# A two-block transformer kernel: the state space mixer's second half is prepared behind the first half's inputs, its pace is halved, and conditioning tiles are spread into GLU and w_out

## The chip, the cores and the metric

The kernel runs on one core of one Trainium2 chip, in one launch. The metric is the device time of that core in microseconds, taken as the median of several executions. The engines are named as the profile names them: PE is TensorE (matmuls and transposes; PEld its weight loads), DVE is VectorE, ACT is ScalarE, POOL is GpSimd, SP is SyncE, which issues the DMAs of the weights. Each works through its own list of instructions in order. A matmul of f32 operands shows in the trace as two passes.

## What is computed

Two transformer blocks follow each other on 256 tokens of width 2048, in f32. The change lies in the first block. Cut to it, the reference is:

```python
mod = silu(c) @ w_ada + b_ada                      # conditioning: 2048 x 12288
shift1, scale1, gate1, shift2, scale2, gate2 = split(mod, 6)
h = rms(x, norm1_w) * (1 + scale1) + shift1
u, q, k, v = split(h @ w_in, 4)                    # in-projection, 1024 columns each
# state space mixer: 64 groups of 16 channels, 64 complex states each
abar = exp((a_re + i a_im) * dt); bbar = (abar - 1) / a * b
h_t = abar * h_(t-1) + bbar u_t                    # over the 256 tokens
y = gelu(Re(c h_t) + d * u)
y_ssm = y * sigmoid(y @ w_glu)                     # GLU, 1024 x 1024
y_att = dilated_attention(rms(q), rms(k), v)       # 8 heads of 128
x = x + gate1 * (concat(y_ssm, y_att) @ w_out)
h2 = rms(x, norm2_w) * (1 + scale2) + shift2
x = x + gate2 * ((silu(h2 @ w_gate) * (h2 @ w_up)) @ w_down)
# the second block (attention mixer, then Fourier mixer) follows
```

## The kernel before

**What it does in which order.** The program is a straight line of instructions that Python writes out. Up to the FFN of the first block it has these stages: load x, norm and first modulation; the in-projection (`turns(ada_group(g), in_tiles(..))`), which reads w_in tile by tile; the evacuation of u (L977); attention, in which `rest(n)` finishes q, k and v, `normed` scales and transposes q and k (L997 to L1006), and `scores` and `values` run eight heads; the attention half of w_out (`gemm_full`, L1072); GLU (`gemm` on `ssm_w_glu`, L1078 to L1089); the SSM half of w_out with the residual (L1101 to L1105); the norm (L1108 to L1116), the second modulation's transposes (`modulated2`, L457) and the FFN.

**Lanes.** Side work is written as Python generators, called lanes. `tick(f)` (L195) adds `f * rate` to each lane's account, and the lane emits pieces until the costs that it yields have used that up. `until(mark)` emits a lane up to a named mark, and `finish()` emits all that is left. So a rate decides how much side work the main line gets between two of its own tiles; each engine then runs its share in the order written. From the evacuation of u to GLU the main line makes 48 ticks: six `rest` calls, eight heads of two half ticks, and 16 tiles of w_out.

**The lane "ada"** brings the conditioning matrix for the later modulations in tiles of 0.5 MB. A first kind (`ada_gen`, loads at L306) is added up on DVE with the token's coefficient (`ada_add`, L278). A second kind (`ada_quad`, loads at L353) goes through PE as four matmuls of 32 rows against `cz` (L133), and is turned by transposes (`ada_turn`, L317). Gate 1 must be there before w_out's residual (`until("g1")`), shift 2 and scale 2 before the FFN (`until("m2")`). Its rate is `T["ada"]` per tick up to GLU and `T["ada2"]` after.

**The lane "ssm"** is the mixer. `products(half)` (L609 to L624) forms powers of abar times bbar on DVE and spreads them by ACT; `expand_b(half)` (L636, L638) transposes them into the input matrices; `outward()` (L647 to L654) prepares c by transposes; `kernel_of(half)` (L664 to L677) multiplies both on PE in 64 passes of 32 columns, then ACT copies the result (L672) and DVE adds d to it (L675, L677). All this needs only parameters, and stands ahead of the mark "prep", at which the lane waits till the in-projection's last group. After u is there, `chunked` (L687) lays it out, `inputs(half)` (L697) makes the input terms with 64 passes of 64 columns, `scan` (L713, L715) runs 63 steps on DVE, `chunk_kernel` (L706) and `outward_powers` (L729 to L737) go along with it, and `outputs` (L753) writes y. Its rate there is `T["ssm"]`.

**Weights.** w_in, w_glu and the SSM half of w_out mostly come through `wtile` (L214): ACT casts the tile to its upper part (L177), DVE subtracts for the lower (L178), and PE makes three products of each. `full_tile` (L207) loads weights that are used as plain f32. Tiles of the lane "ada" and of `wtile` share one set of five buffers, `raw`, and SP's queue.

In the changed kernel lines from 765 on stand one or more lines further down (L1002 there is L1001 here).

Of the kernel before, what the change touches and what calls it, by code (L numbers as in the profile page):

```python
# [20 lines left out]
A_SCALE = 192.0 ** -0.5  # L21
B_SCALE = 128.0 ** -0.5
TWO_PI = 6.283185307179586
T = dict(groups=((0, 2), (2, 6), (6, 10), (10, 14), (14, 16)), db=(0, 6), us=(3,4),qs=(), hf=0.5, raw=5, sl=14, side=[[0, 1, 2, 3], [0, 1, 2, 3], [0, 1, 2], [0, 1, 2], []], ada0=0.0, ada=1.8, ssm0=0.6, ssm=5, md=(2, 2), ld=(3, 3), stg=(7, 7), r1=(0, 0), ada2=0.2, prep=1.6, hb=0.75, ha=1.5, cx=0.6)


class Act:
# [54 lines left out]
def kernel(ctx: ExitStack, tc: tile.TileContext, A, out):  # L82
# [20 lines left out]
    def slab(shape, dt=F32):  # L103
        return sl.tile(shape, dt, name=uname("sl"), tag="sl", bufs=NSLAB)
# [398 lines left out]
    def ssm():  # L503
# [94 lines left out]
        exs, kst, bls, us = {}, {}, {}, {}  # L598

        def products(half):  # L600


            pr = slab([128, 4, 256])
            ex = exs[half] = [w8([128, 16, 4, 2, 16]) for _ in range(2)]
            f = lambda a: a.rearrange("p (g c) -> p g c", c=16)

            def cmul(dr, di, ar, ai, br, bi):
                t1 = temp()
                V.tensor_tensor(out=f(dr), in0=f(br), in1=by_pair(ar, half), op=ALU.mult)  # L609
                V.tensor_tensor(out=f(t1), in0=f(bi), in1=by_pair(ai, half), op=ALU.mult)  # L610
                V.tensor_tensor(out=dr, in0=dr, in1=t1, op=ALU.subtract)
                V.tensor_tensor(out=f(di), in0=f(bi), in1=by_pair(ar, half), op=ALU.mult)
                V.tensor_tensor(out=f(t1), in0=f(br), in1=by_pair(ai, half), op=ALU.mult)
                V.tensor_tensor(out=di, in0=di, in1=t1, op=ALU.add)
            for j in range(4):
                d = [pr[:, 2 * (j % 2) + comp] for comp in range(2)]
                if j == 0:
                    cmul(*d, sm[:, 2], sm[:, 3], bb[:, half, 0], bb[:, half, 1])
                else:
                    cmul(*d, sm[:, 0], sm[:, 1], *last)  # L620
                last = d
                for comp in range(2):
                    for g in range(2):
                        S.activation(out=ex[comp][:, :, 3 - j, g], in_=f(d[comp]), func=AF.Copy,  # L624
                                     scale=maskb[:, g:g + 1])
                yield 2.0

        def expand_b(half):

            bls[half] = []  # L630
            for comp in range(2):
                bt = w8([128, 16, 128])
                for q in range(4):
                    b = ps_tp()
                    for i in range(4):
                        PE.transpose(b[:, i * 128:(i + 1) * 128],  # L636
                                     exs[half][comp][:, 4 * q + i].rearrange("p j g c -> p (j g c)"), ident)
                    S.copy(bt[:, 4 * q:4 * q + 4].rearrange("p g n -> p (g n)"), b)  # L638
                bls[half].append(bt)
                yield 0.5  # L640

        def outward():

            for comp in range(2):
                for half in range(2):
                    cx = w2([128, 4, 2, 64], "wb")
                    S.activation(out=cx, in_=cn[:, comp, 4 * half:4 * half + 4].unsqueeze(2).to_broadcast([128, 4, 2, 64]),  # L647
                                 func=AF.Copy, scale=(1.0, -1.0)[comp])
                    b = ps_tp()
                    for kk in range(4):  # L650
                        PE.transpose(b[:, kk * 128:(kk + 1) * 128], cx[:, kk].rearrange("p g n -> p (g n)"), ident)
                    for g in range(2):
                        r_ = slice(64 * g, 64 * g + 64)
                        S.copy(gc[r_, comp, 16 * half:16 * half + 16],  # L654
                               b[r_].rearrange("p (k g c) -> p k g c", g=2, c=16)[:, :, g])
                    yield 0.5

        def kernel_of(half):

            ct = []  # L660
            for comp in range(2):
                ct.append(w2([128, 16, 2, 16], "wb"))
                for g in range(2):
                    S.activation(out=ct[comp][:, :, g], in_=gc[:, comp, 16 * half:16 * half + 16], func=AF.Copy,  # L664
                                 scale=maskb[:, g:g + 1])
            b = ps_at()
            for q in range(16):
                for comp in range(2):
                    mm(b[:, 32 * q:32 * q + 32], exs[half][comp][:, q].rearrange("p j g c -> p (j g c)"),
                       ct[comp][:, q].rearrange("p g c -> p (g c)"), comp == 0, comp == 1)  # L670
            k = kst[half] = sp.tile([128, 16, 32], F32, name=uname("ssm_k"), tag="ssm_k", bufs=2)
            S.copy(k.rearrange("p q n -> p (q n)"), b)  # L672
            l0 = slice(96, 128)
            dd = w2([128, 16, 32], "wb")
            V.tensor_tensor(out=dd[l0], in0=ident[l0, 96:128].unsqueeze(1).to_broadcast([32, 16, 32]),  # L675
                            in1=dcol[l0, 16 * half:16 * half + 16].unsqueeze(2).to_broadcast([32, 16, 32]), op=ALU.mult)
            V.tensor_tensor(out=k[l0], in0=k[l0], in1=dd[l0], op=ALU.add)  # L677
            yield 2.0

        def chunked(half):  # L680

            us[half] = slab([128, 16, 64])
            for i in range(4):
                for q in range(4):
                    d = us[half][32 * i:32 * i + 32].rearrange("p (k q) n -> p q k n", q=4)[:, q]
                    copy = (S.copy, V.tensor_copy)[q % 2]
                    copy(d, uT[half][32 * q:32 * q + 32, :, i:256:4])  # L687

        def inputs(half):

            for comp in range(2):
                for h8 in range(2):
                    b = ps_at()
                    for q in range(8):
                        mm(b[:, q * 64:(q + 1) * 64], bls[half][comp][:, 8 * h8 + q], us[half][:, 8 * h8 + q], True, True)
                    g0 = 16 * half + 8 * h8
                    S.copy(st[:, :, comp, g0:g0 + 8].rearrange("p n g -> p g n"), b.rearrange("p (g n) -> p g n", g=8))  # L697
# [22 lines left out]
        def outward_powers():  # L720

            for half in range(2):
                gx[half] = [w8([128, 16, 4, 2, 16]) for _ in range(2)]
                gr, gi = (gc[:, comp, 16 * half:16 * half + 16] for comp in range(2))
                ar, ai = by_pair(sm[:, 0], half), by_pair(sm[:, 1], half)
                f = lambda a: a.rearrange("p (g c) -> p g c", c=16)
                for j in range(4):
                    t1, t2 = temp(), temp()
                    V.tensor_tensor(out=f(t1), in0=gi, in1=ai, op=ALU.mult)  # L729
                    V.tensor_tensor(out=f(t2), in0=gr, in1=ai, op=ALU.mult)  # L730
                    V.tensor_tensor(out=gr, in0=gr, in1=ar, op=ALU.mult)
                    V.tensor_tensor(out=gi, in0=gi, in1=ar, op=ALU.mult)
                    V.tensor_tensor(out=gr, in0=gr, in1=f(t1), op=ALU.add)
                    V.tensor_tensor(out=gi, in0=gi, in1=f(t2), op=ALU.subtract)
                    for comp, g_ in enumerate((gr, gi)):
                        for g in range(2):
                            S.activation(out=gx[half][comp][:, :, j, g], in_=g_, func=AF.Copy, scale=maskb[:, g:g + 1])  # L737
                    yield
# [19 lines left out]
        dcol = tmp[:, 0]  # L758
        for q in range(4):
            V.tensor_copy(dcol[96:128].rearrange("p (k q) -> p q k", q=4)[:, q], colv[32 * q:32 * q + 32, C_D:C_D + 8])  # L760
        gc = slab([128, 2, 32, 16])
        yield from outward()
        for half in range(2):
            yield from products(half)
            yield from kernel_of(half)
            if half == 0:
                yield from expand_b(0)
        yield "prep"

        st = sp.tile([128, 64, 2, 32], F32, name=uname("ssm_h"), tag="ssm_h", bufs=2)  # L770
# [1 line left out]
        for i in range(1, 4):  # L772
            G.memset(tk[32 * i:32 * i + 32, :, :, 0:i].rearrange("p h q j c -> p (h q) (j c)"), 0.0)
        chunked(0)
        inputs(0)
        yield 1.0
        chunked(1)
        yield from expand_b(1)
        inputs(1)
        powers = outward_powers()  # L780
        yield 1.0
        for c, cost in enumerate(scan()):
# [1016 lines left out]
```

## Time and profile before

| | us |
|---|---|
| median of three runs | 2521.72 |
| lowest and highest of them | 2508.95, 2525.09 |
| the profiled execution | 2516.57 |
| its span | 2514.6 |
| its mean granted clock of PE | 0.975 |

The rows are read from the profiled execution. Times within it count from the start of its span. A row of windows gives, for a stretch, the busy time of each engine with its number of instructions, PE's granted clock as a share of full speed (2.4 GHz; 0.50 is the lower level), and the load of DMA. The chain of waits follows the work that ended last back through what released it.

### The profile page before, as it was taken

How to read it: one execution, taken by the hardware profiler on the slowest of the kernel's cores; microseconds unless marked ns; L12 is line 12 of the kernel's file. 1: busy time of each engine (PE TensorE's matmuls, PEld its weight loads, DVE VectorE, ACT ScalarE, POOL GpSimd, SP SyncE). 2: the span in 40 equal slices, each digit the busy share in tenths (PEclk: the TensorE clock that was granted, in tenths of full speed). 3: DMA queues.
4: the chain of work that ended last, by engine and by line, in shares of the span. 5: the costliest groups of instructions: out<-in, count | busy, mean ns of one | idle time of the engine just before them, and what ended most of it. 6: DMA issues, size and time to landing. Idle time of an engine off the chain costs nothing.

```text
span 2514.6 us, 30153 instructions
## 1 busy us (share of the span) xinstructions
PE 2379.3 (95%) x10791; PEld 1826.3 (73%) x10791; DVE 1768.4 (70%) x2809; ACT 1127.4 (45%) x1770; POOL 5.6 (0%) x7
## 2 busy tenths in 40 slices
PE   5899999989999999999999999999997999999997
PEld 3456645567888778778777878777776778888886
DVE  5876795477668899886777789645678655555557
ACT  3334835355444333434345464555444445444442
POOL 0000000000000000000000000000000000000000
PEclk9888999999999999999999999999998999999999
DMA  9867587877888888888777998634473765665664
GB/s 291 307 241 268 192 300 244 287 253 258 282 272 289 279 290 287 272 257 276 260 250 229 294 302 282 216 102 149 126 261 108 229 212 173 190 198 156 176 209 139
DMA packets 291535, 591.32 MB, mean 235 GB/s; under 512 B 33733, under 2 KB 56617, under 8 KB 291385
## 3 DMA queue, kind: packets, MB, share of 16 engines
q1 hardware_dynamic: 291384, 589.40, 72.1%
q8 instruction: 84, 1.38, 0.2%
q14 instruction: 67, 0.54, 0.1%
HBM read 587.19 MB, written 2.13 MB: 234 GB/s over the span
## 4 chain that ended last, share of the span: by engine, by line
PE 52%; DVE 20%; DMA 18%; issue 5%; ACT 4%; SPq 0%; DVEq 0%; ACTq 0%
PE mm L133 41%; DMA raw<-in_ada_w_dram 14%; PE at L133 7%; DVE wl L178 6%; DVE acc L278 6%; PE tp L133 2%; ACT wh L177 1%; DMA raw<-in_w_ada_dram 1%; DMA raw<-in_w_ffn_down_dram 1%; DMA raw<-in_w_in_attn_dram 1%; PE tp L189 1%; DVE ssm_h L715 1%; DVE wa L278 0%; DVE sl L1570 0%; DVE sl L1573 0%
## 5 line engine op out<-in xcount | busy, mean ns | idle before, releaser
L133 PE MATMUL mm<-wh,s 128*128 128x512 f32 (+3 forms) x4768 | 1464.8, 386 | 2.5 <-ACT wh L177 2.2
L177 ACT CAST wh<-raw 128x1024 fp32r<-128x1024 f32 (+3 forms) x642 | 655.8, 1023 | 900.3 <-PE mm L133 653.4
L133 PEld LDWEIGHTS mm<-wh,s 128*128 128x128 f32 x4768 | 891.4, 189 | 181.8 <-issue 8.6
L178 DVE TENSOR_TENSOR wl<-raw,wh 128x1024 fp32r<-128x1024 f32 (+3 forms) x642 | 756.3, 1186 | 321.0 <-ACT wh L177 319.3
L133 PE MATMUL mm<-wl,s 128*128 128x512 f32 (+3 forms) x2384 | 923.3, 387 | 23.2 <-DVE wl L178 21.4
L278 DVE SCALAR_TENSOR_TENSOR acc<-raw,condT,acc 128x1024 f32<-128x1024 f32 (+2 forms) x413 | 477.7, 1165 | 235.9 <-DMA raw<-in_ada_w_dram 146.4
L133 PEld LDWEIGHTS mm<-wl,s 128*128 128x128 f32 x2384 | 451.3, 189 | 124.6 <-DVE wl L178 38.9
L133 PE MATMUL mm<-wh,sl 128*128 128x512 f32 x536 | 196.2, 459 | 4.5 <-ACT sl L817 2.8
L133 PE MATMUL mm<-wl,sl 128*128 128x512 f32 x440 | 194.9, 521 | 4.3 <-DVE wl L178 2.3
L133 PEld LDWEIGHTS mm<-wh,sl 128*128 128x128 f32 x536 | 100.5, 191 | 56.5 <-issue 32.4
L133 PEld LDWEIGHTS mm<-wl,sl 128*128 128x128 f32 x440 | 82.2, 193 | 68.5 <-issue 51.3
L133 PE MATMUL tp<-wc,sl 128*128 128x128 f32 (+1 forms) x352 | 49.3, 293 | 20.0 <-ACT wc L901 15.3
L133 PEld LDWEIGHTS tp<-wc,sl 128*128 128x128 f32 x352 | 44.9, 199 | 29.8 <-ACT wc L901 15.6
L278 DVE SCALAR_TENSOR_TENSOR wa<-raw,condT,wa 128x512 f32<-128x512 f32 (+1 forms) x75 | 48.2, 642 | 10.1 <-DMA raw<-in_w_ada_dram 9.3
L133 PE MATMUL at<-wl,sl 128*128 128x512 f32 x112 | 52.4, 617 | 0.5 <-DVE sl L864 0.5
L133 PE MATMUL at<-s,s 128*128 128x512 f32 (+1 forms) x96 | 44.8, 647 | 3.9 <-ACT wd L1381 3.3
L133 PEld LDWEIGHTS at<-wl,sl 128*128 128x128 f32 x112 | 21.3, 198 | 26.6 <-issue 21.5
L133 PE MATMUL at<-wh,sl 128*128 128x512 f32 x80 | 36.0, 597 | 0.0
L457 PE MATMUL tp<-ident,sl 128*128 128x128 f32 x64 | 12.0, 337 | 22.7 <-ACT sl L1594 10.5
L189 PEld LDWEIGHTS tp<-ident,wa 128*128 128x128 f32 x208 | 24.5, 141 | 10.4 <-issue 3.3
L189 PE MATMUL tp<-ident,wa 128*128 128x128 f32 x208 | 30.5, 276 | 0.0
L715 DVE TENSOR_TENSOR ssm_h<-ssm_h,ssm_tq 128x64 f32<-128x64 f32 x126 | 27.6, 219 | 1.4
(345 smaller groups left out, 1725.2 us busy)
## 6 DMA issues: line engine op xcount, KB each, us to landing
raw<-in_w_ada_dram SPq DMA_DIRECT2D x192, 512.0 KB, 5.3
raw<-in_ada_w_dram SPq DMA_DIRECT2D x192, 512.0 KB, 4.6
raw<-in_w_in_fourier_dram SPq DMA_DIRECT2D x128, 512.0 KB, 4.1
raw<-in_w_ffn_gate_dram SPq DMA_DIRECT2D x88, 512.0 KB, 4.9
raw<-in_w_ffn_up_dram SPq DMA_DIRECT2D x88, 512.0 KB, 4.7
raw<-in_w_ffn_down_dram SPq DMA_DIRECT2D x88, 512.0 KB, 5.6
raw<-in_w_in_attn_dram SPq DMA_DIRECT2D x72, 512.0 KB, 5.1
raw<-in_w_out_fourier_dram SPq DMA_DIRECT2D x64, 512.0 KB, 4.0
```

The costliest lines, as they stand in the source:

```text
L133: PE.matmul(o, l, r, start=start, stop=stop)
L177: S.copy(hi, src)
L178: V.tensor_sub(lo, src, hi.bitcast(F32))
L189: PE.transpose(b[:, o:o + 128], src(c0 + c, t), ident)
L278: V.scalar_tensor_tensor(out=acc, in0=raw, scalar=c, in1=acc, op0=ALU.mult, op1=ALU.add)
L457: PE.transpose(b[:, c * 128:(c + 1) * 128], xn(4 * g + c, t), ident)
L715: V.tensor_tensor(out=cur, in0=cur, in1=tq[:, :, i], op=ALU.add)
```

## The change

Three rates are changed in the table T: `ada` 1.8 to 1.6, `ssm` 5 to 2.4, `ada2` 0.2 to 0.85. In the lane "ssm" only `products(0)` and `expand_b(0)` stay ahead of the mark "prep". `outward`, `kernel_of(0)`, `products(1)` and `expand_b(1)` now follow `inputs(0)`, and `kernel_of(1)` follows `inputs(1)`. The layout of u for each half yields a cost of 2.0.

```diff
-T = dict(..., ada0=0.0, ada=1.8, ssm0=0.6, ssm=5, ..., ada2=0.2, ...)
+T = dict(..., ada0=0.0, ada=1.6, ssm0=0.6, ssm=2.4, ..., ada2=0.85, ...)
...
-        gc = slab([128, 2, 32, 16])
-        yield from outward()
-        for half in range(2):
-            yield from products(half)
-            yield from kernel_of(half)
-            if half == 0:
-                yield from expand_b(0)
+        yield from products(0)
+        yield from expand_b(0)
         yield "prep"
...
         chunked(0)
+        yield 2.0
         inputs(0)
-        yield 1.0
+        gc = slab([128, 2, 32, 16])
+        yield from outward()
+        yield from kernel_of(0)
+        yield from products(1)
+        yield from expand_b(1)
         chunked(1)
-        yield from expand_b(1)
+        yield 2.0
         inputs(1)
+        yield from kernel_of(1)
         powers = outward_powers()
         yield 1.0
```

How this moves instructions shows at three places.

ACT in the kernel before, in the in-projection, around the copy L672 of the first kernel's result (`at` is its bank, `ssm_w` a table of `products` or `expand_b`, L817 and L177 prepare the modulated inputs of the in-projection):

```order
L624 ACTIVATE ssm_w_148_674<-sl_146_672,maskb_110 128x16x16 x2
L817 ACTIVATE sl_42_195<-sl_42_195,col_3_95,col_4_96 128x256 x2
L817 ACTIVATE sl_45_208<-sl_45_208,col_3_95,col_4_96 128x256 x2
L177 CAST ssm_h_13_114<-sl_42_195 128x512
L177 CAST ssm_h_13_114<-sl_45_208 128x512
L672 COPY ssm_k_188_899<-at_187_866 128x512
L664 ACTIVATE wb_259_1263<-sl_129_601,maskb_110 128x16x16 x2
L638 COPY ssm_w_199_944<-tp_200_945 128x512
```

ACT in the changed kernel, in attention, around the same copy (L1002 scales q or k, L1007 evacuates their transposes, L654 is part of `outward`):

```order
L647 ACTIVATE wb_301_1418<-sl_59_279 128x512
L1002 ACTIVATE sl_86_359<-sl_86_359,rhy_314_1483 128x128
L654 COPY sl_268_1301<-tp_300_1411 64x256 x2
L664 ACTIVATE wb_303_1427<-sl_268_1301,maskb_110 128x16x16 x2
L654 COPY sl_268_1301<-tp_302_1420 64x256 x2
L664 ACTIVATE wb_304_1430<-sl_268_1301,maskb_110 128x16x16 x2
L1002 ACTIVATE sl_86_359<-sl_86_359,rhy_314_1483 128x128 x2
L1002 ACTIVATE sl_86_359<-sl_86_359,rhy_323_1513 128x128 x4
L672 COPY ssm_k_306_1466<-at_305_1433 128x512
L1007 ACTIVATE sl_326_1533<-tp_327_1534,colv_79 128x512
```

The copy stood behind the modulation of inputs and ahead of the first expansion; it now stands behind the scaling of keys and ahead of the evacuation of their transposes.

SP's queue of DMAs in the kernel before, at the start of GLU (L214 are tiles of w_glu, L353 and L306 conditioning tiles):

```order
L306 DMA raw_713_3231<-in_w_ada_dram 128x1024
L214 DMA raw_720_3248<-in_ssm_w_glu_dram 128x2x512
L214 DMA raw_723_3266<-in_ssm_w_glu_dram 128x2x512
L214 DMA raw_726_3284<-in_ssm_w_glu_dram 128x2x512
L353 DMA raw_729_3302<-in_w_ada_dram 128x2x512
L214 DMA raw_730_3304<-in_ssm_w_glu_dram 128x2x512
L214 DMA raw_742_3345<-in_ssm_w_glu_dram 128x2x512
```

The same place in the changed kernel:

```order
L306 DMA raw_700_3183<-in_w_ada_dram 128x1024
L214 DMA raw_707_3200<-in_ssm_w_glu_dram 128x2x512
L353 DMA raw_710_3222<-in_w_ada_dram 128x2x512
L214 DMA raw_711_3224<-in_ssm_w_glu_dram 128x2x512
L306 DMA raw_714_3242<-in_w_ada_dram 128x1024
L214 DMA raw_715_3245<-in_ssm_w_glu_dram 128x2x512
L353 DMA raw_718_3263<-in_w_ada_dram 128x2x512
L214 DMA raw_719_3265<-in_ssm_w_glu_dram 128x2x512
```

From GLU to the end of w_out there were 9 conditioning tiles and are 21; before GLU there were 87 and are 77.

PE in the kernel before, from the last products of w_out (`wh`, `wl`) over the norm's transposes (L457) to the first FFN product (`s2`; `acc` with `e0` sums a conditioning tile of the first kind):

```order
L133 MATMUL mm_822_3719<-wh_833_3752,sl_761_3438 128x512
L133 MATMUL mm_704_3196<-raw_769_3467,cz_111 32x512 x2
L133 MATMUL mm_704_3196<-raw_813_3684,cz_111 32x512 x2
L133 MATMUL tp_857_3864<-acc_668_3059,e0_91 32x512 x2
L133 MATMUL mm_704_3196<-raw_854_3857,cz_111 32x512
L317 MATMUL tp_859_3869<-ident_75,wc_858_3867 128x64 x4
L133 MATMUL mm_704_3196<-raw_856_3862,cz_111 32x512 x2
L317 MATMUL tp_861_3882<-ident_75,wc_860_3880 128x128 x4
L457 MATMUL tp_870_3902<-ident_75,sl_843_3818 128x128 x4
```

The same place in the changed kernel:

```order
L133 MATMUL mm_825_3731<-wh_845_3805,sl_755_3420 128x512
L457 MATMUL tp_874_3926<-ident_75,sl_855_3879 128x128 x4
L457 MATMUL tp_876_3938<-ident_75,sl_855_3879 128x128 x4
L457 MATMUL tp_878_3950<-ident_75,sl_856_3880 128x128 x4
L133 MATMUL mm_882_3974<-wh_885_3978,s2_866_3918 128x512
L457 MATMUL tp_880_3962<-ident_75,sl_856_3880 128x128 x4
```

The conditioning matmuls and their transposes are gone from between w_out and the norm's transposes; the narrow ones against `cz` that stood there, and part of those that stood in attention, are now among GLU's and w_out's products.

## Rows read from the trace of the kernel before

**Rows 1.** The page: busy time, share of the span, instructions of each engine.

```profile
PE 2379.3 (95%) x10791; PEld 1826.3 (73%) x10791; DVE 1768.4 (70%) x2809; ACT 1127.4 (45%) x1770; POOL 5.6 (0%) x7
```

**Rows 2.** Windows by stage: length; busy PE, PEld, DVE, ACT, POOL; clock; DMA share, GB/s.

```profile
148.00:234.00 86.00, 79.75 (x321) 53.26 (x320) 59.10 (x105) 28.66 (x61) 0.00 (x0) 0.85 0.69 235
234.00:300.00 66.00, 63.40 (x278) 42.97 (x277) 46.74 (x160) 56.84 (x130) 5.41 (x3) 0.88 0.59 204
300.00:427.00 127.00, 121.73 (x530) 65.95 (x530) 101.85 (x340) 59.64 (x153) 0.00 (x0) 1.00 0.79 273
427.00:476.00 49.00, 49.00 (x153) 19.39 (x153) 13.64 (x17) 9.22 (x20) 0.00 (x0) 1.00 0.85 296
476.00:551.30 75.30, 72.28 (x316) 55.47 (x310) 52.95 (x57) 35.21 (x45) 0.00 (x0) 1.00 0.78 251
551.30:564.30 13.00, 7.63 (x45) 3.93 (x45) 12.38 (x43) 11.09 (x23) 0.00 (x0) 0.84 0.85 296
```

**Rows 3.** The chain of waits, 140 to 300 us: start, us, what.

```profile
148.27 24.41 PE at L133 x96
...
221.47 9.53 PE at L133 x64
...
248.93 12.48 PE at L133 x60
...
263.23 0.95 PE tp L636 x8
```

**Rows 4.** The timeline of PE from 155 us: start, us, instructions.

```profile
155.06 8.62 PE L133 MATMUL at<-wb,ssm_w 128*128 128x32 f32 x64
163.49 1.20 PE L133 MATMUL at<-wl,sl 128*128 128x512 f32 x1
```

**Rows 5.** Windows around the narrow matmuls, and one in attention.

```profile
160.00:164.00 4.00, 4.00 (x23) 3.97 (x23) 0.69 (x1) 0.28 (x1) 0.00 (x0) 0.61 0.08 31
164.00:172.50 8.50, 8.50 (x16) 3.39 (x15) 6.90 (x10) 2.01 (x5) 0.00 (x0) 0.78 0.55 169
226.00:231.00 5.00, 5.00 (x25) 5.00 (x25) 0.39 (x1) 0.00 (x0) 0.00 (x0) 0.50 0.06 24
231.00:236.00 5.00, 5.00 (x12) 3.93 (x13) 4.75 (x5) 1.28 (x3) 0.00 (x0) 0.51 0.00 0
...
255.00:261.20 6.20, 6.20 (x31) 6.20 (x31) 2.45 (x3) 2.80 (x4) 0.00 (x0) 0.50 0.79 291
...
300.00:325.00 25.00, 24.54 (x84) 13.39 (x84) 25.00 (x87) 14.05 (x32) 0.00 (x0) 1.00 0.83 278
```

**Rows 6.** Waits up to 234 us: who for whom: us in total, times, longest.

```profile
ACT ssm_k L672 <- PE at L133: 45.7, 2, 33.1
...
DVE wb L675 <- PE at L133: 12.5, 2, 6.5
```

**Rows 7.** The timeline of PE around one set of narrow conditioning matmuls.

```profile
357.99 1.07 PE L133 MATMUL mm<-raw,cz 128*32 128x512 f32 x8
358.99 0.70 PE L133 MATMUL mm<-wl,sl 128*128 128x512 f32 x1
```

**Rows 8.** DVE's groups, 234 to 476 us (busy, mean ns | idle), and line L609.

```profile
L278 DVE SCALAR_TENSOR_TENSOR acc<-raw,condT,acc 128x1024 f32<-128x1024 f32 x51 | 64.8, 1278 | 40.9 <-DMA raw<-in_w_ada_dram 40.7
...
L609 DVE TENSOR_TENSOR sl<-sl,ssm_cols x8: 417/420/429, 102.3 to 183.9; 128x256 f32<-128x256 f32 x8
```

**Rows 9.** The timeline of PE in the tail, with idle before and its releaser.

```profile
551.31 1.07 PE L133 MATMUL mm<-raw,cz 128*32 128x512 f32 x8
...
556.17 0.66 PE L317 MATMUL tp<-ident,wc 128*128 128x128 f32 x4 [0.72 <-ACT wc L314]
558.03 1.27 PE L457 MATMUL tp<-ident,sl 128*128 128x128 f32 x8 [1.20 <-ACT sl L1116]
562.75 1.94 PE L457 MATMUL tp<-ident,sl 128*128 128x128 f32 x8 [3.45 <-DVE wa L462]
564.34 0.78 PE L133 MATMUL mm<-wh,s 128*128 128x512 f32 x1
```

## Prediction before the run

> **What bounds the kernel now.** I read the page first. TensorE (PE) is busy 95% of the span [rows 1], so a change pays only where PE waits, or where its clock is low. Then I cut the part that the change touches into stages [rows 2]: the in-projection (A, until 234 us), attention with the SSM scan and the attention half of w_out (B, 234 to 476), GLU and the SSM half of w_out (C, 476 to 551.3), and the tail up to the first FFN matmul (551.3 to 564.3). PE is busy 72.28 of 75.3 us in C, 121.73 of 127 in the middle of B, all 49 in its last part. Only the tail is open: 7.63 of 13.0. From 564 us on nothing is changed, so I take the time after it as it was.
>
> The chain of waits [rows 3] shows that the pieces to be moved are PE work on the path: `kernel_of(0)` is the end of the piece at 148.27, `kernel_of(1)` is the 9.53 us piece at 221.47, `inputs(0)` the 12.48 us piece at 248.93. All are narrow matmuls (32 or 64 columns) that follow each other without a gap. The timeline has the first kernel as 64 passes from 155.06 to 163.49, 8.4 us [rows 4].
>
> Third, the clock. From 160 to 164 PE is busy 4.00 of 4.00 us, and the granted clock is 0.61; from 226 to 231 it is busy all 5 us at 0.50 [rows 5]. The wide matmuls behind them inherit the low clock: 0.78 over 8.5 us, 0.51 over 5 us. The same happens to `inputs(0)`, 0.50 from 255 to 261.2. So PE falls to its lower level (1.2 GHz) while it does narrow work, not when it idles.
>
> **The change, part by part.**
>
> *A loses two kernels and the outward transposes.* The kernels are 8.4 us [rows 4] and 9.5 us [rows 3]. Sixteen transposes of `outward` are priced by the same form of transpose elsewhere, 0.95 us for 8 [rows 3], so 1.9 us. Together 19.8 us. The wide matmuls behind the kernels also get their clock back: 8.5 × 0.22 = 1.9 us and 5 × 0.49 = 2.4 us [rows 5], 4.3 us. **A: −24.1.** ACT's 45.7 us and DVE's 12.5 us of waiting for the kernels [rows 6] go too, but PE was never idle behind them, so I price that at nothing; its cover is the queue of in-projection matmuls. If that cover were gone, the price would be the third rival's.
>
> *B gets the same work.* At the full clock the kernels would be 17.9 less 4 × 0.39 and 5 × 0.50 (the shares of [rows 5]), so 13.8 us, and with the transposes 15.7. At the half clock throughout they are twice that, 31. B's own narrow work in the same style, `inputs(0)`, fell to 0.50 with PE fully busy, and `kernel_of(1)` now follows `inputs(1)` directly. So I take what the kernels cost in A, 19.8, and half of the aftermath, 2.2: **+22** (bounds +15.7 and +31).
>
> The Trainium skill ("TensorE: Matmul & The Clock Gate", section "Why this matters for your kernels") ties the fall of the clock to idle gaps of PE between bursts of matmuls. By that rule the moved kernels would run at full clock in B, where PE has no gaps, and the sum would be 6 us lower than mine; the clock of 0.61 with PE busy 4.00 of 4.00 speaks against it here.
>
> *Fewer conditioning tiles in B.* The lane's pace falls from 1.8 to 1.6 per tick, and by the instruction order 77 tiles are issued before GLU, where there were 87. Of the narrow conditioning matmuls 41 stand in B on PE, before 54. Four of them take 1.00 us in the timeline, from 357.99 to 358.99 [rows 7], so 0.25 each: 13 × 0.25 = **−3.3**.
>
> *DVE in B.* `products(1)` brings 24 operations of 0.42 us [rows 8], 10.1 us, and the two kernels a block each. Against that, the scan's 63 steps are handed out at less than half the pace. They now run from 275 on, in the stretch where DVE is busy 25.00 of 25 us [rows 5], beside 51 conditioning adds of 1.28 us that wait 40.9 us in all for their tiles [rows 8]. PE idles 5.3 us from 300 to 427 [rows 2]; a flatter load should return part of it. Bounds 0 and −5.3; I take **−2**.
>
> *The wait at the top of the queues.* ACT stands still at L672 until PE has done the kernel, 33.1 us at the longest [rows 6], and DVE at L675 up to 6.5. In the new order L672 on ACT comes behind all eight `L1002` scalings of the keys, so what PE needs next is done before ACT blocks. Price nothing; what hides it is PE's queue, in which `inputs`, transposes and 512-column products are in line.
>
> *GLU and w_out get twelve more tiles.* There were 9 and are 21, 0.5 MB each. On PE that is 21 more narrow matmuls (23, were 2): 21 × 0.25 = 5.3 us, since PE is busy 72.28 of 75.3 us [rows 2]. This is the lower bound. On DVE six or so more adds of 1.28 us fit into 22 idle us. For DMA: C moved 251 GB/s × 75.3 = 18.9 MB and would move 25.2. At 296 GB/s, the rate of B's last part with the same mixture of weights and tiles [rows 2], that is 85 us, 9.8 more than now: the upper bound. I take **+7**, nearer the lower one, because DMA at 251 GB/s is a consequence of PE's pace now.
>
> *The tail.* Before, eight narrow conditioning matmuls, two summing ones and eight turning transposes stand between the last w_out matmul and the norm's transposes [rows 9], and then the transposes wait 1.20 us for ACT and 3.45 us for DVE. In the new order none of that stands there, and the first FFN matmul comes ahead of the last transposes. What stays is the norm itself. From 551.31 to 558.03 there are 6.7 us of conditioning work on PE and behind it; but the row chain on DVE and ACT (sum of squares, reciprocal root, scaling) runs meanwhile. At least the 0.72 us idle goes, at most 5. I take **−4**. The matmuls that leave it are paid in C.
>
> The sum: −24.1 + 22 − 3.3 − 2 + 7 − 4 = −4.4 us. The profiled execution took 2516.6 us (span 2514.6 and 2 us around it), so the result is **2512 us**. The runs shown have a median of 2521.7, 0.2% above; I keep to the profiled one.
>
> **The rivals.**
>
> *The moved work vanishes in B (faster).* If the kernels, spread between wide matmuls, run at the full clock (+15.7), PE's idle 5.3 us in B goes entirely, `inputs(0)` is freed of half its low clock (6.2 × 0.50 = 3.1 us), C pays only PE's 5.3 and the tail gives 5: −24.1 + 15.7 − 3.3 − 5.3 − 3.1 + 5.3 − 5 = −19.8, **2497 us**. For it: B has clock 1.00 from 300 on. Against: `kernel_of(1)` still stands behind `inputs(1)` as one narrow block of 128 passes. The Trainium skill ("Perfetto Trace Analysis", section "Optimization Strategy") says that interleaving regimes with different limits can gain; PE being the limit in A, in B and in C alike [rows 2], there is little here to interleave.
>
> *C becomes bound by DMA.* If C's rate stays at 251 GB/s [rows 2], 25.2 MB take 100 us, 25 more than now instead of 7: −4.4 + 18 = +14, **2530 us**. It decides as soon as the tiles come at less than 25.2 MB / 80.6 us = 313 GB/s. For it: in the new order of the DMA queue a conditioning tile stands between every two weight tiles from the start of GLU. Against: B's last part, mixed in the same way, kept PE busy 49.00 of 49 us at 296.
>
> *DVE becomes the bound in B (slower than before).* `products(1)`, 10.1 us, and two blocks of 6.25 us at L675 [rows 6, 8] now fall into a stage in which DVE is full for 25 us at a stretch [rows 5] and feeds the softmax. If all of it is passed on, 22.6 us: −4.4 + 22.6 = +18, **2535 us**. It decides if these stand where DVE has no idle time left; against it speaks that 427 to 476 has DVE busy only 13.64 of 49 us [rows 2], and that the scan, which filled the full stretch, is spread out.
>
> That the change does nothing of what it says is excluded by the instruction order: kernels, tiles and tail stand elsewhere. The costs that the mixer's lane yields behind its mark add up to about 88, at 2.4 per tick 37 of the 48 ticks there are before GLU, so its rest does not pile up there.
>
> **How the numbers follow.** My forecast has 0.5 (own range 2503 to 2521), the faster rival 0.2, C bound by DMA 0.15, DVE 0.1, anything else 0.05. The range that leaves out no more than 0.2 runs from 2492 to 2534. A measurement of this kernel tells a difference of about 1%, 25 us, from none. Under 2496 lie half of the first rival and some of the rest, 0.18; over 2547 only DVE and C together or something unseen, 0.06; between them 0.76.
>
> **What would show it.** Right: A ends 20 to 26 us earlier with clock 1.00 where the kernels stood, B is 13 to 20 us longer with low clock at both kernels, C is 80 to 85 us, the tail about 9. Wrong: kernels in B at clock 1.00 (first rival); PE in C idle behind splits L178 that wait for `raw` tiles (second); DVE at 100% for more than 50 us in B with PE waiting for L1018 to L1031 (third); or A not shorter, because the group boundaries of the modulation, not PE, set its end.

## The result, and the profile after

The changed kernel takes 2533.4 us (median of 20 runs, 2520.74 to 2543.2) against 2512.74 us of the kernel before (20 runs), and the ratio of the means is 1.0072, 95% interval 1.0054 to 1.0089, so it is some 18 us slower. The forecast was 2512 us and 4 us faster. The time lies just inside the wider range, outside the forecast's own (2503 to 2521), and on the other side of no change.

Both profiled executions are cut at the same four events: the first copy of u out of PSUM (ACT), the last copy of w_out's attention half (ACT), the start of the last residual's first operation on DVE, and, on PE, the start of the last of the norm's 16 transposes for the first half of the tokens. The lengths between them, here and in the tables below, are differences of start times in the trace:

| us | A: up to u | B: attention | C: GLU and w_out | tail | sum |
|---|---|---|---|---|---|
| before | 234.6 | 241.1 | 76.1 | 12.5 | 564.3 |
| changed | 207.7 | 270.2 | 93.8 | 14.1 | 585.7 |
| difference | -26.9 | +29.1 | +17.7 | +1.6 | +21.4 |
| forecast | -24.1 | +16.7 | +7 | -4 | -4.4 |

So A gave what was forecast, and three terms behind it came out too small. What follows on the tail took 1950.4 us before and 1947.9 us in the changed kernel, so the spans differ by 19.0. Over all profiled executions of this document that rest lies between 1939 and 1950 us: a difference of a few us between two spans says little by itself.

The windows by stage of the changed kernel, in the columns of [rows 2]:

```profile
207.70:300.00 92.30, 88.37 (x428) 63.16 (x427) 58.71 (x143) 64.06 (x145) 5.41 (x3) 0.85 0.60 212
300.00:406.00 106.00, 103.67 (x408) 53.48 (x407) 90.87 (x362) 51.40 (x143) 0.00 (x0) 1.00 0.75 261
406.00:477.90 71.90, 70.45 (x240) 39.21 (x238) 23.09 (x40) 22.75 (x49) 0.00 (x0) 0.86 0.57 184
477.90:506.60 28.70, 28.43 (x126) 19.53 (x125) 18.19 (x19) 14.21 (x17) 0.00 (x0) 1.00 0.77 265
506.60:570.70 64.10, 58.45 (x244) 37.53 (x242) 45.37 (x55) 26.20 (x42) 0.00 (x0) 1.00 0.86 290
570.70:585.70 15.00, 3.90 (x16) 3.35 (x17) 14.49 (x39) 8.19 (x15) 0.00 (x0) 0.58 0.84 267
```

Three things stand out. The last part of attention, which had clock 1.00 and PE busy throughout [rows 2], has 0.86; the second half of the SSM outputs, which stood ahead of that part before, now stands in it. And in w_out, from 506.6 on, PE is idle 5.7 of 64.1 us. In the tail PE has lost half its work (3.90 us, before 7.63), but DVE is busy 14.49 of 15.0 us, and the stage is no shorter.

Finer windows of the changed kernel show where the clock is low in B: at the end of `inputs(0)` (222), in `kernel_of(0)` (252) and the wide matmuls behind it (258), in `kernel_of(1)` (288) and behind it (294), and in the second half of the SSM outputs (411), though not in the first (394):

```profile
222.00:226.00 4.00, 4.00 (x21) 4.00 (x21) 1.08 (x1) 1.75 (x5) 0.00 (x0) 0.50 0.99 367
252.00:258.00 6.00, 6.00 (x32) 6.00 (x32) 0.48 (x1) 0.12 (x1) 0.00 (x0) 0.53 0.77 302
258.00:263.00 5.00, 5.00 (x12) 2.72 (x11) 3.66 (x10) 4.72 (x11) 0.00 (x0) 0.54 0.00 0
288.00:294.40 6.40, 6.40 (x40) 6.40 (x40) 0.20 (x1) 0.10 (x1) 0.00 (x0) 0.65 0.00 1
294.40:300.00 5.60, 5.60 (x8) 2.50 (x9) 5.31 (x15) 3.86 (x7) 0.00 (x0) 0.50 0.43 135
394.30:404.40 10.10, 10.10 (x92) 10.10 (x91) 2.66 (x5) 1.14 (x3) 0.00 (x0) 1.00 0.98 363
...
411.30:430.40 19.10, 19.08 (x96) 19.10 (x97) 3.88 (x8) 4.63 (x8) 0.00 (x0) 0.54 0.30 101
```

The kernels and their aftermath are as forecast. The outputs are not: 92 passes in 10.1 us, then 96 of the same kind in 19.1 us, with PE busy all the while.

What the low clock takes of B in all can be estimated from one window over the whole of it, as its length times what the clock lacks to 1.00. First the kernel before, then the changed one:

```profile
234.60:475.70 241.10, 233.23 (x955) 127.73 (x956) 161.48 (x514) 125.40 (x302) 5.41 (x3) 0.97 0.75 260
207.70:477.90 270.20, 262.49 (x1073) 155.85 (x1071) 172.67 (x544) 138.21 (x336) 5.41 (x3) 0.91 0.65 224
```

That is some 7 us before and 24 us in the changed kernel, so about 17 of the 29 us by which B grew are low clock. PE's idle time in B did not change (7.9 and 7.7 us).

In C the waits of ACT for weights have grown. Here is the row of the kernel before (476 to 552 us), in the columns of [rows 6]:

```profile
ACT wh L177 <- DMA raw<-in_w_out_dram: 5.9, 3, 3.3
```

And that of the changed kernel (478 to 571 us):

```profile
ACT wh L177 <- DMA raw<-in_w_out_dram: 30.7, 11, 5.6
```

Its chain of waits, in the columns of [rows 3], tells how a weight comes to be late:

```profile
501.95 4.86 DMA raw<-in_w_ada_dram
...
506.90 1.29 DVE acc L278
508.22 6.13 DMA raw<-in_w_out_dram
...
514.43 1.05 ACT wh L177
515.51 1.24 DVE wl L178
```

A conditioning tile lands after 4.9 us, DVE adds it up, only then is its buffer free, and a tile of w_out is issued into that buffer and lands 6.1 us later. ACT, then DVE, wait for exactly this tile. Fetching is no longer ahead of use.

### The profile page after: what moved, and what is told of

It reads as the page before. It is cut to its first block, busy times and chain, and to the rows that moved or that the text cites. A ratio compares the mean times of both kernels' runs of the same rounds, so it can differ in the third digit from the quotient of the medians.

```text
span 2533.6 us, 30150 instructions
## 1 busy us (share of the span) xinstructions
PE 2386.6 (94%) x10791; PEld 1828.3 (72%) x10791; DVE 1770.2 (70%) x2809; ACT 1126.1 (44%) x1767; POOL 5.6 (0%) x7
## 4 chain that ended last, share of the span: by engine, by line
PE 53%; DMA 20%; DVE 18%; issue 4%; ACT 4%; SPq 1%; DVEq 0%; ACTq 0%
PE mm L133 42%; DMA raw<-in_ada_w_dram 14%; PE at L133 6%; DVE wl L178 5%; DVE acc L278 5%; DMA raw<-in_w_ada_dram 3%; PE tp L133 2%; ACT wh L177 1%; DMA raw<-in_w_in_attn_dram 1%; DMA raw<-in_w_ffn_gate_dram 1%; PE tp L189 1%; DMA wl<-in_w_in_dram 1%; DVE sl L1571 0%; DVE sl L1574 0%; DMA raw<-in_w_out_dram 0%
## 5 line engine op out<-in xcount | busy, mean ns | idle before, releaser
L177 ACT CAST wh<-raw 128x1024 fp32r<-128x1024 f32 (+3 forms) x642 | 656.2, 1023 | 945.2 <-PE mm L133 699.9
L133 PE MATMUL mm<-wh,sl 128*128 128x512 f32 x560 | 210.9, 472 | 5.4 <-ACT sl L818 2.8
L133 PE MATMUL mm<-wl,sl 128*128 128x512 f32 x416 | 182.9, 515 | 3.4 <-DVE wl L178 3.2
L457 PE MATMUL tp<-ident,sl 128*128 128x128 f32 x64 | 12.5, 349 | 28.7 <-ACT sl L1595 10.5
L189 PEld LDWEIGHTS tp<-ident,wa 128*128 128x128 f32 x208 | 24.4, 140 | 13.2 <-issue 3.8
L457 PEld LDWEIGHTS tp<-ident,sl 128*128 128x128 f32 x64 | 9.9, 180 | 31.3 <-ACT sl L1595 11.0
```

Of the source, the lines that this page charges most:

```text
L133: PE.matmul(o, l, r, start=start, stop=stop)
L177: S.copy(hi, src)
L189: PE.transpose(b[:, o:o + 128], src(c0 + c, t), ident)
L457: PE.transpose(b[:, c * 128:(c + 1) * 128], xn(4 * g + c, t), ident)
```

## The experiments

The result gave three questions: what the tiles do in C, what the tail hangs on, and why B is 12 us longer than forecast. First the change was taken apart into its rates and its order. All ratios are against the kernel before on the same chip, with 95% intervals.

**Only the tile rates undone** (`e1_tiles_back`).

```diff
-ada=1.6, ssm=2.4, ada2=0.85
+ada=1.8, ssm=2.4, ada2=0.2
```

> The changed kernel with the two conditioning rates set back (ada 1.8, ada2 0.2): the mixer's new order and pace stay. Theory (twelve more tiles in GLU and w_out starve PE of weights there, about +17 us in that stage and its tail): that stage is 75 to 77 us long again, the in-projection stays 27 us shorter, attention 20 to 30 us longer, so the total is within -8 to +4 us of the kernel before. Rival (the tiles are innocent, the stage is longer because the mixer's work comes late): GLU and w_out stay at 90 us and more, total +14 to +20.

**Only the new order** (`e2_order_only`): as above, and `ssm=5`.

> As e1, and the mixer's pace also back at 5: only the new order of its preparation is left. Theory on attention (the second block of SSM outputs falls to the low clock because the two blocks now stand close to each other, not because of the pace): the blocks stand four wide matmuls apart here too, so one of them is at half clock, attention is 25 to 32 us longer, total 0 to +8 against before. Rival (the halved pace is what moves the outputs to a bad place): with pace 5 attention is only 14 to 20 us longer, total -8 to -14.

**Only the tile rates, on the kernel before** (`e3_tiles_only`).

```diff
-ada=1.8, ada2=0.2
+ada=1.6, ada2=0.85
```

> The kernel before with only the two conditioning rates of the change (ada 1.6, ada2 0.85). Theory (tiles starve PE in GLU and w_out): that stage takes 90 to 94 us instead of 75.3, the tail is not shorter, attention 3 us shorter; total +10 to +18. Rival of the prediction (7 us in the stage, 4 off the tail): total within +-3.

**Only the pace, on the kernel before** (`e4_pace_only`): `ssm=5` to `ssm=2.4`.

> The kernel before with only the mixer's pace at 2.4. Theory (outputs crowd together behind the heads and fall to the low clock): attention +4 to +10 us, the other stages as before, total +4 to +10. Rival (a flatter scan relieves DVE and costs nothing): total -4 to 0.

| kernel | ratio (interval) | A | B | C | tail |
|---|---|---|---|---|---|
| e1_tiles_back | 1.0029 (1.0010 to 1.0049) | 211.4 | 278.6 | 79.2 | 12.0 |
| e2_order_only | 1.0059 (1.0034 to 1.0083) | 209.2 | 279.1 | 78.3 | 12.2 |
| e3_tiles_only | 1.0070 (1.0041 to 1.0100) | 235.1 | 245.9 | 94.5 | 14.1 |
| e4_pace_only | 0.9995 (0.9973 to 1.0017) | 234.9 | 242.9 | 77.6 | 11.9 |

The tiles are guilty in C: with them C is 94 us with or without the mixer's new order, without them 78 to 79. The rates alone cost as much as the whole change (e3, at the upper end of what was expected). The pace alone costs nothing, as its rival had it. The order costs too: in e1 and e2 B grows by 38 us, where A shrinks by 23 to 25. That is more than expected, and so both missed in the total as well (some 7 and 15 us slower than before, where -8 to +4 and 0 to +8 were expected). With the old tile rate PE runs dry between the heads. In the window below it was busy 11.38 of 12 us in the changed kernel; in `e1_tiles_back` it is

```profile
378.00:390.00 12.00, 7.17 (x31) 4.19 (x30) 11.03 (x42) 3.66 (x10) 0.00 (x0) 0.80 0.92 311
```

PE waits there for a conditioning tile and then for DVE; that is read from the trace, and no run takes the two apart. Over the whole of B, PE is idle 12.3 us in e1:

```profile
211.50:490.10 278.60, 266.32 (x1099) 154.62 (x1097) 180.75 (x552) 138.81 (x337) 5.41 (x3) 0.92 0.67 233
```

My expectation for e2, that the outputs would be at half clock with the old pace, failed: they ran at full clock there (10.1 and 10.6 us), and B was long all the same. With the new order the lower tile rate shortens B by 8 us (e1 against the changed kernel) and lengthens C by 15.

**Which cost of a tile: its transfer, its place, or its work?** In `e5_no_tile_dma` the tiles of C keep their buffers and their work, but are not transferred (`part[0]` is set from GLU to the end of w_out; the edit is the same at both loads):

```diff
-            SY.dma_start(raw, W[...])
+            if part[0]:
+                G.memset(raw, 0.0)
+            else:
+                SY.dma_start(raw, W[...])
```

> The changed kernel, but from GLU to the end of w_out a conditioning tile is not loaded: GpSimd writes zeros into its buffer, and the buffer, the DVE add and the PE matmuls stay (so shift 2 and scale 2 are wrong in part). Theory (PE starves because the transfer of tiles stands ahead of that of weights): GLU and the SSM half of w_out, 93.8 us between the last copy of w_out's attention half and the last residual of it, shrink to 79 to 84, the total by 10 to 15 us against the changed kernel, so about +3 to +8 against before. Rival (PE's matmuls, DVE's adds and the order they impose are the cost): 90 us or more, total +15 and more.

In `e6_own_buffers` they keep their transfer, but not the places of the weights:

```diff
+    def ada_raw(shape):
+        if part[0]:
+            t = sp.tile([128, 2048], F32, name=uname("ssm_w"), tag="ssm_w", bufs=4)
+            return t[:, 0:1024].rearrange("p (k n) -> p k n", k=shape[1])
+        return wp.tile(shape, F32, name=uname("raw"), tag="raw", bufs=NRAW)
```

> The changed kernel, but from GLU to the end of w_out the conditioning tiles go into four buffers of their own (the mixer's tables, free by then) and no longer take places among the five that the weights use. All bytes are still moved. Theory (it is the places: with a tile between every two weights the weights are fetched one or two tiles ahead and no longer four): the stage shrinks from 93.8 to 80 to 86 us, total +5 to +10 against before. Rival (bandwidth: 25 to 27 MB in the stage are too much): 90 us or more, total +15 and more.

**The tail without adds** (`e7_no_tiles_in_tail`): `db=(0, 6)` to `db=(6, 6)`, the account with which the lane "ada" starts behind w_out.

> The changed kernel with the conditioning lane held back for six units behind w_out, so that its three adds (1.28 us each) no longer stand in DVE's list among the norm's operations. Theory (the tail is set by what stands ahead of the norm on DVE): the time from the last residual to the last transpose of the norm, 14.1 us, falls to 9 to 11. Rival (the norm's chain itself takes that long): 13 to 15. In the total a change of 4 us at most, +14 to +18 against before.

**The kernels left out** (`e8_no_kernels`): in `kernel_of` two matmuls of 128x512 in place of 32 narrow ones.

> The changed kernel with each kernel_of's 32 narrow matmuls left out and two wide ones of 128x512 in their place (1.7 us each; the mixer's output is wrong). It prices the moved work in attention. Theory (the kernels run at the low clock there and leave it to the wide matmuls behind): attention, 270.2 us from the first copy of u to the last copy of w_out's attention half, falls by 19 to 22 us; total -1 to -4 against before. Rival (the clock would be low there in any case, or other work fills the gap): it falls by 10 to 12 us, total +6 to +8.

| kernel | ratio (interval) | A | B | C | tail |
|---|---|---|---|---|---|
| e5_no_tile_dma | 1.0051 (1.0027 to 1.0074) | 208.0 | 272.2 | 86.8 | 16.1 |
| e6_own_buffers | 1.0017 (0.9986 to 1.0048) | 206.8 | 277.9 | 81.2 | 16.3 |
| e7_no_tiles_in_tail | 1.0038 (1.0013 to 1.0064) | 207.5 | 261.9 | 93.2 | 11.9 |
| e8_no_kernels | 0.9987 (0.9964 to 1.0010) | 208.2 | 248.7 | 95.6 | 14.1 |

In e5 and e6 a part of C moved over its border into the tail, so C and tail are to be read together: 107.9 us in the changed kernel, 102.9 without transfers, 97.5 with own buffers, 88.6 before. e5 came out between its two expectations, e6 as the theory of places had it: the places weigh more than the transfers. ("Places" covers two things that no run takes apart: e6 has nine buffers in all where the changed kernel has five, and its weights share theirs with nothing.) With own buffers ACT waits for PE in C, not for weights (484 to 572 us):

```profile
ACT wh L177 <- PE mm L133: 22.5, 13, 3.6
```

Without the transfers but with shared places it still waits for the tiles of w_out (480 to 571 us):

```profile
ACT wh L177 <- DMA raw<-in_w_out_dram: 22.6, 11, 4.5
```

The changed kernel's rate in C was no ceiling either: it moved 284 GB/s there, and e6 304 GB/s with PE busy 80.24 of 81.1 us. Here is C of the one, then of the other:

```profile
477.90:571.60 93.70, 86.88 (x367) 57.06 (x366) 64.46 (x75) 41.26 (x60) 0.00 (x0) 1.00 0.83 284
484.70:565.80 81.10, 80.24 (x358) 58.23 (x358) 60.49 (x70) 40.24 (x58) 0.00 (x0) 0.98 0.88 304
```

e8 was to price the moved kernels. Attention is 21.5 us shorter without them, as expected, and some 3.4 us of wide matmuls stood in for them, which would make 25 us. But part of that is luck: in the profiled execution of e8 all outputs ran at the full clock, and the second block took 10.9 us where the changed kernel's took 19.1:

```profile
384.50:394.80 10.30, 10.30 (x94) 10.27 (x92) 2.82 (x5) 2.11 (x5) 0.00 (x0) 1.00 0.84 321
400.10:411.00 10.90, 10.86 (x97) 10.89 (x98) 3.93 (x8) 4.64 (x8) 0.00 (x0) 1.00 0.53 173
```

Against e7, whose outputs ran at the full clock too, e8's B is 13.2 us shorter, so the kernels cost 17 us by this pair. In A they and their aftermath were priced at 22.2. The move by itself bought a few us at most.

e7 took 2.2 us off the tail, less than expected: the FFN's splits still stand there. That B was 8 us shorter in it than in the changed kernel, with the same order of PE up to GLU, is the clock: the second half of its outputs took 10.6 us at 1.00.

```profile
412.60:423.20 10.60, 10.59 (x95) 10.60 (x96) 3.90 (x8) 4.64 (x8) 0.00 (x0) 1.00 0.56 180
```

Its total, too, is 8 us below the changed kernel's, when the tail gives 2. The granted clock of every timed run tells why. Span times what the mean clock lacks to 1.00 is an estimate of what the low clock takes of a run, and what is left of the span is an estimate of its time at the full clock (means over the runs, us):

| kernel | runs | low clock | at full clock |
|---|---|---|---|
| before (beside four groups of runs) | 23 to 31 each | 63 to 67 | 2450 |
| changed | 20 | 67 | 2462 |
| e1_tiles_back | 10 | 60 | 2461 |
| e3_tiles_only | 6 | 71 | 2461 |
| e5_no_tile_dma | 10 | 68 | 2458 |
| e6_own_buffers | 10 | 67 | 2453 |
| e7_no_tiles_in_tail | 10 | 61 | 2462 |
| e8_no_kernels | 10 | 52 | 2459 |
| f1_buffers_and_tail | 12 | 63 | 2451 |
| g5_outputs_apart | 12 | 63 | 2461 |
| g1_all_mends | 12 | 61 | 2451 |

(f1, g1 and g5 follow below.) e7 equals the changed kernel at the full clock, and most of its gain is low clock; why that was rarer in its runs stays open, and the tail's 2 us do not show in the total. The changed kernel lies 12 us above the kernel before at the full clock, and own buffers take 9 of them back. The low clock takes only 1 to 4 us more in the changed kernel than before.

**Both mends together, and crosses of them.** `f1_buffers_and_tail` joins e6 and e7. `f2_buffers_no_dma` joins e6 and e5. `f3_before_tiles_buffers` gives the kernel before the new tile rates with both mends, `f4_before_buffers` both mends alone.

> The changed kernel with both mends: conditioning tiles from GLU to the end of w_out go into four buffers of their own, and none are added up behind w_out until six units of the FFN have passed. Theory (places and tail are what the change lost beyond attention): GLU and w_out 83 to 86 us (96.5 in the changed kernel, 77.5 before), tail 9 to 11, total -4 to +5 against before. Rival (the mends only move the loss on into the FFN): total +10 and more.

> As the run with four own buffers, and the tiles from GLU to the end of w_out again not loaded but zeroed by GpSimd (shift 2 and scale 2 wrong in part). It asks what the transfer itself costs once places are not short. If bandwidth still counts: GLU and w_out 80 to 82 us against 84.8 with the transfers. If only PE's narrow matmuls are left (5.3 us): 83 to 85.

> The kernel before, its mixer untouched, with the change's conditioning rates, four own buffers from GLU on and no adds behind w_out for six units. Theory (places cost 12 us of the 18 that the rates alone cost): total +2 to +8 against before, GLU and w_out 83 to 86 us. Rival (own buffers help only together with the new order): +13 and more.

> The kernel before with its own rates, only with four own buffers for the nine tiles from GLU on and no adds behind w_out for six units. With nine tiles places are hardly short: GLU and w_out 74 to 77 us (77.5 before), tail 9.5 to 11, total -4 to 0. If places were short there too, 72 us and -6.

| kernel | ratio (interval) | A | B | C | tail |
|---|---|---|---|---|---|
| f1_buffers_and_tail | 0.9987 (0.9961 to 1.0013) | 208.7 | 272.7 | 80.7 | 10.6 |
| f2_buffers_no_dma | one run only | 208.3 | 272.1 | 79.1 | 14.1 |
| f3_before_tiles_buffers | 1.0007 (0.9980 to 1.0033) | 236.3 | 240.9 | 82.9 | 10.6 |
| f4_before_buffers | 1.0007 (0.9981 to 1.0033) | 237.0 | 252.6 | 73.1 | 12.8 |

The expectations count C up to the last residual's third operation; by that border it took 82.2 us in f1, 82.7 in f2 (between its two cases), 84.4 in f3 and 74.6 in f4. f4 is the kernel to set beside f1 and f3, since it has both mends too. With both, twelve more tiles cost 5.4 us over C and tail in f1 (91.3 against 85.9) and 7.6 in f3 (93.5). f2 has the adds in the tail, so it belongs beside e6: leaving the transfer out takes C and tail from 97.5 to 93.2 us. So the transfers are worth 4 to 5 us with shared buffers (e5) and with own ones (f2), and the places 10 us with the transfers (e6) and without them (f2 against e5); each of these is a difference of two single executions. Bandwidth was the smaller part. f3 says the same without the new order: the tile rates that cost 0.7% cost nothing measurable with both mends.

**The outputs set apart** (`g5_outputs_apart`, and `g1_all_mends` on top of f1): in `outputs`

```diff
-                yield 2.0
+                yield 4.8
```

> The changed kernel with one number changed: each of the four groups of outputs yields a cost of 4.8 instead of 2.0, so that the second pair of groups (48 passes each) has eight wide matmuls between its members and no longer stands as 96 passes in a row. Theory (96 narrow passes soon after 92 others let the clock fall): all four groups run at 0.11 us a pass, attention takes 258 to 263 us instead of 270.2, total +8 to +12 against before. Rival (the clock falls there whatever the order): one group or two still at 0.2 us a pass, attention 268 to 274, total +15 and more.

> The changed kernel with own buffers for the conditioning tiles from GLU on, no adds behind w_out for six units, and the outputs set apart as in the run beside it. Theory: in-projection -27, attention +18 to +22, GLU with w_out and tail +2 to +4 (they were +2.7 with the two first mends), so -2 to -8 against before, ratio 0.997 to 0.999. Rival (outputs keep the half clock): as with the two first mends, ratio 0.9985 to 1.001.

| kernel | ratio (interval) | A | B | C | tail |
|---|---|---|---|---|---|
| g5_outputs_apart | 1.0041 (1.0018 to 1.0063) | 208.7 | 260.1 | 93.0 | 14.1 |
| g1_all_mends | 0.9991 (0.9971 to 1.0012) | 208.9 | 266.8 | 80.7 | 10.6 |

In both all outputs ran at 0.11 us a pass, with the clock at 1.00 wherever they stand; here g1 in the stretch that was at 0.54:

```profile
411.30:431.00 19.70, 19.70 (x104) 12.60 (x104) 10.43 (x22) 9.25 (x21) 0.00 (x0) 1.00 0.49 158
```

B is 10 us shorter in g5 than in the changed kernel, and the total 0.3%. g1's B is longer again, in part because its two kernels ran at 0.18 and 0.19 us a pass, where the changed kernel's had 0.15 and 0.14. None of these kernels is measurably faster than the kernel before; g1 and f1 equal it and are 0.8% faster than the changed one. With f1 at 0.9987 and g1 at 0.9991, setting the outputs apart shows no gain on top of the two other mends.

## Why the prediction was wrong, step by step

**A, -24.1: right**, and a little small (-26.9).

**The same work in B, +22: right in mechanism and nearly in size.** Late in the kernels the clock was 0.53 and 0.65, and in the wide matmuls behind them 0.54 and 0.50, with PE busy 6.00 of 6 us. The Trainium skill ("TensorE: Matmul & The Clock Gate", section "Why this matters for your kernels") looks for a drop in idle gaps of PE between bursts of matmuls. No gap stands in these windows, so the trace does not bear that out here. It does in the tail, and the prediction's "not when it idles" went too far: PE is busy 3.90 of 15.0 us there, at a mean clock of 0.58. e8 puts the price of the kernels in B at 17 to 25 us, by which kernel it is set against; the sixteen transposes, 1.9 us, come on top.

**What B lost beyond that, 0 in the forecast, was 8.5 us of low clock:** the second block of the SSM outputs, 19.1 us where e7's took 10.6. I took it that only the moved work changes its clock, and this term was missing from the sum. Without it B is +20.8 (e7) and +19.0 (g5), against +16.7 forecast. But it is not shown that the change causes it. With its order five executions of six have the second block at the low clock. With the old order two of four have the first block there (e3 and f4): f4, with the order of the kernel before up to GLU, has a B of 252.6 us where that kernel's profiled execution has 241.1. That the two blocks stand close is not enough: they are 6.6 us apart in the changed kernel, 4 to 5 us in e2 and e8, and there both ran at the full clock. What decides stays open, and the means over the timed runs give the low clock only 1 to 4 us of the 18.

**Fewer tiles in B, -3.3: too small where the mixer's order is new.** By e1 and the changed kernel it is 8 us. I had counted only PE's time for 13 matmuls. PE's idle time between the heads went with the tiles, 12.3 us in e1 against 7.7. Against e7, whose outputs ran at the full clock as e1's did, the difference is 17 us, but some 7 of these are low clock in other narrow work (0.92 over e1's B, 0.94 over e7's), which nothing ties to the tiles.

**DVE in B, -2: came to nothing.** PE's idle time in B stayed as it was (7.9 and 7.7 us). That is also what the wait at the top of the queues, priced at nothing, cost.

**C, +7: wrong, this is the largest error** (+17.7). The upper bound, 9.8, was worked out from the bytes at the best rate of a neighbouring stage. The bound that held was another: five buffers that weights and tiles share. With a tile between every two weights these have about half of the places. The prediction knew that order, but took from it only the bytes. The rival "C becomes bound by DMA" came near in time (2530), but by luck. It was worked out from 251 GB/s, and C ran at 284. That is under the 313 which the rival names, but as a consequence of the places: e6 moved its tiles at 304 with PE busy throughout, and leaving the transfers out gave 4 to 5 us where giving places gave 10. The two terms that the forecast did have were about right: with both mends on either side the twelve tiles cost C and tail 5.4 us (f1 against f4) and 7.6 (f3 against f4), between the forecast's bounds of 5.3 and 9.8. The term that was missing is the places, 10 us.

**The tail, -4: wrong** (+1.6). The step that failed is that the norm's chain "runs meanwhile" beside PE. [rows 2] had DVE busy 12.38 of the 13.0 us. Taking PE's work away left DVE's, and the new order put more in. The timeline of DVE in the changed kernel:

```profile
570.31 0.15 DVE L1109 TENSOR_REDUCE s<-ssq 128x1 f32<-128x4 f32 x1
570.38 1.28 DVE L278 SCALAR_TENSOR_TENSOR acc<-raw,condT,acc 128x1024 f32<-128x1024 f32 x1
...
572.29 1.22 DVE L178 TENSOR_TENSOR wl<-raw,wh 128x1024 fp32r<-128x1024 f32 x1
...
575.06 1.22 DVE L178 TENSOR_TENSOR wl<-raw,wh 128x1024 fp32r<-128x1024 f32 x1
...
576.44 1.28 DVE L278 SCALAR_TENSOR_TENSOR acc<-raw,condT,acc 128x1024 f32<-128x1024 f32 x1
...
579.31 1.27 DVE L278 SCALAR_TENSOR_TENSOR acc<-raw,condT,acc 128x1024 f32<-128x1024 f32 x1
...
581.30 0.88 DVE L1115 TENSOR_SCALAR sl<-sl,ry 128x512 f32<-128x512 f32 x2
```

Three adds of the next gate's tiles and two splits of FFN weights, 6.3 us, stand between the norm's first reduction and its scaling on DVE; in the kernel before it was one of each, 2.5 us. PE meanwhile has nothing (its timeline):

```profile
579.21 1.97 PE L457 MATMUL tp<-ident,sl 128*128 128x128 f32 x8 [8.54 <-ACT sl L1117]
```

Without the adds (e7) this wait is shorter:

```profile
569.04 1.97 PE L457 MATMUL tp<-ident,sl 128*128 128x128 f32 x8 [6.48 <-ACT sl L1117]
```

A part of the forecast's 4 us is there once the adds are away: the tail takes 12.8 us with PE's conditioning work in it (f4) and 10.6 without it (f1, f3, g1).

**The rival with DVE as the bound of B** did not come: 300 to 406 us had DVE at 91 of 106 us and PE at 104.

So the change moved work from one stage that PE fills to another, at not much less than its old price, and paid on top for tiles that took places from weights (10 us in e6) and for DVE work put ahead of the norm (2 us of the tail in e7). In the profiled execution it paid as well for outputs at the half clock (8.5 us), which the kernel before can meet too. With the first two mended (f1) it equals the kernel before.

## What to carry to other kernels

When a stream of side tiles shares a set of buffers with the weights, count places as well as bytes: how many tiles ahead are the weights still fetched? Free memory of a finished stage can give the side stream buffers of its own. Moving work between two stages that the same engine fills gains little by itself, so look there for what else the move shifts. Where the granted clock differs between executions of one order, set executions with like clocks beside each other before a stage's difference is put down to an edit. Before a stage is credited with a term on one engine, look which engine is busy in it: a tail with DVE at 95% was not shortened by taking matmuls out of it while DVE's work grew.

## What was not expected of the hardware

The granted clock of one block of narrow matmuls differs between executions of one order: 96 passes took 10.6 us in e7 and 18.6 to 19.1 us in five others (the changed kernel, e5, e6, f1 and f2), with PE busy throughout. Where the outputs were spread further they took 0.11 us a pass in all four executions profiled (e1, e4, g1, g5), although in e1 and e4 up to 96 passes still stood nearly together.
